# An attention stage whose tensor-engine order is written out by hand

## The chip, the cores and the metric

The kernel runs on one core of a Trainium2 chip. The metric is device microseconds of one launch. Engines are named as the profile names them: PE (matmul), DVE (vector), ACT (scalar), POOL (GpSimd) and SP, which issues the DMAs.

## What is computed

Two groups of tokens, a prompt of 1024 and a sample of 64 with a past of 512 keys, pass through two layers that share weights. The layer that matters here is the even one:

```python
q, k, v, ga, qi, ki, wi, gb, gc, xin, gz = split(h @ w_in)
score = sum_h wi[h] * relu(qi[h] @ ki.T)            # 8 index heads
keep  = the topk best keys of each query             # 256 for the prompt, 144 for the sample
p     = softmax(where(keep, q @ k.T / 8, -inf))      # 8 heads of 64, 2 key heads
a_out = (p @ v) * silu(ga)
b_out = gb * conv3(gc * xin) * silu(gz)
x    += gate * (concat(a_out, b_out) @ w_out)
```

A prompt query may see the keys of its own 64-chunk and of those before it. The odd layer (a gated projection, layer norm, a spatial product) follows and is not touched.

## The kernel before

Activations lie with features on the 128 partitions and all `TC` = 1088 tokens (1024 prompt, 64 sample) along the row. Every product is made of fp32r parts: a weight tile is split into `hi` and `lo` (ACT L238, POOL L239), the input into `ah` and `al`, and `project`/`steps` run three matmuls for each of 8 input tiles. With the three chunks of `CHUNKS` (364, 364 and 360 columns) one weight tile is 72 matmuls.

The work around the change, in order of the program:

- `topk` (DVE and ACT) finds each query's threshold for 7 score blocks `j`: six prompt blocks of 128 queries (b = 2 to 7, with 128(b+1) keys) and the sample's (576 keys). `mask` (L592 to L607, DVE but for one ACT step) then writes a block's additive bias into `self.bias`, through the scratch tile `self.cum`. Both live in the pool `search`.
- The pool `attn` opens when `search` closes, in the same memory. It holds the sample's keys `kc`, the query stacks `qst` (hi and lo parts of two heads, made by `pair_stack`: ACT L698, POOL L699), the parts `pth`/`ptl` of transposed probabilities (two buffers each) and the gate `ga`.
- Four head pairs `t` are attended, each in eight prompt blocks `b` (`ORDER[t]`) and the sample. `softmax` makes logits in chunks of at most 512 columns (PE L620), adds the bias and takes the maximum (DVE L622), exponentiates with a row sum (ACT L625), takes the reciprocal (DVE L626) and scales (POOL L627). `weighted` takes two key tiles at a time: four PE transposes into a PSUM bank (L650), the split into `pth` (ACT L276) and `ptl` (DVE L277), and the products with the values (PE L658). At the end of a block ACT copies the lower half out (L662) and DVE adds it (L722).
- Beside this run 11 projection tiles (`ATTN_TILES`: Q 1 to 3, GB 0 to 3, GA 0 to 3). They come from the generator `self.side`, one matmul at a time (PE L262): `BEFORE` = 435 of them ahead of the attention, then some at each `pace` call. A GA tile must wait until its head pair is done (`while kind == GA and self.done <= t: yield`): its evacuation copies the gate (ACT L909), applies Silu (L911) and multiplies into `self.q` (POOL L912), or for the last pair does it by chunks (L905, L906).
- Then `self.q` and `self.bo` are split into `ah`, `al` (L276, L277) and `out_projection` starts (PE L247, tile `op`).

PE, DVE, ACT and POOL each run their queue in order. A planner writes the order of all queues, by its own estimate of times and the order of the program; `pace` ties a few filler matmuls behind a given instruction (`issue_after`). PSUM has eight banks: `pj` 2, `lg` 3, `pt` 2, `av` 1.

Of the kernel before, what the change touches and what calls it, by code (L numbers as in the profile page):

```python
# [9 lines left out]
F32 = mybir.dt.float32  # L10
# [38 lines left out]
ATTN_TILES = [(Q_, 1), (Q_, 2), (Q_, 3), *((GB, t) for t in range(4)), *((GA, t) for t in range(4))]  # L49
# [38 lines left out]
BEFORE = 435  # L88
RATE = ((1, 1, 2),) * 4
# [8 lines left out]
class Trunk:  # L98
    def __init__(self, tc, ins, outs):
        self.tc, self.nc = tc, tc.nc  # L100
        self.i, self.o = ins, outs
        self.tags = ["pj"]

# [6 lines left out]
    def bank(self, tag, name):  # L110

        return self.ps.tile([P, 512], F32, tag=tag, name=name, bufs={"pj": 2, "lg": 3, "pt": 2, "av": 1}[tag])
# [137 lines left out]
    def steps(self, w, evac, chunks=range(NCH), n=2, tag="pj"):  # L250
# [3 lines left out]
        for c in chunks:  # L254
            a, b = CHUNKS[c]
            ps = self.bank(tag, "pj")[:, 0:b - a]
# [230 lines left out]
    def topk(self, pool):  # L487
# [11 lines left out]
        self.kneg = kneg = t("kneg")  # L499
# [11 lines left out]
        cv, m, sgn, limx, T, cand, flag = (t(n) for n in ("cv", "m", "sgn", "limx", "T", "cand", "flag"))  # L511
        self.T, self.cv, self.sgn = T, cv, sgn
        junks = [self.cum, pool.tile([P, SEQ], BF, name="junk")]
# [78 lines left out]
    def mask(self, pool, j):  # L592
# [14 lines left out]
        V.tensor_scalar(bi, bi, MASK, None, op0=OP.mult)  # L607


    def softmax(self, slot, lhs, keys, g, n, bias):  # L610

        nc = self.nc
        k, w = cut(n)
        p = self.S[:, slot:slot + n]
        st = self.small.tile([P, 4], F32, tag="sm", name="sm", bufs=8)
        for c in range(k):
            s = slice(c * w, (c + 1) * w)
            pt = self.bank("lg", "logit_ps")
            for i in range(2):
                mm = nc.tensor.matmul(pt[:, 0:w], lhs, keys[i][:, g, s], start=i == 0, stop=i == 1)  # L620
            self.pace(mm.ins, self.rate[0])
            nc.vector.tensor_tensor_reduce(out=p[:, s], in0=pt[:, 0:w], in1=bias[:, s], scale=-0.125,  # L622
                                           scalar=st[:, c - 1:c] if c else 3.0e38, op0=OP.add, op1=OP.min,
                                           accum_out=st[:, c:c + 1])
        nc.scalar.activation(p, p, AF.Exp, scale=-1.0, bias=st[:, k - 1:k], accum_out=st[:, 2:3])  # L625
        nc.vector.reciprocal(st[:, 3:4], st[:, 2:3])  # L626
        nc.gpsimd.tensor_scalar(p, p, st[:, 3:4], 0.0, op0=OP.mult, op1=OP.add)  # L627
        return p

    def weighted(self, pool, ps, g, n, vbase):  # L630

        nc = self.nc
        m = len(ps) * P
        av = self.bank("av", "av")
        nj = (n + P - 1) // P
        step = 512 // m
        for j0 in range(0, nj, step):
            js = range(j0, min(j0 + step, nj))
            full = [j for j in js if (j + 1) * P <= n]
            pt = self.bank("pt", "p_ps")  # L640
            hi = pool.tile([P, 512], F32R, tag="pth", name="pth", bufs=2)
            lo = pool.tile([P, 512], F32R, tag="ptl", name="ptl", bufs=2)
            for part in (full, [j for j in js if j not in full]):
                if not part:
                    continue
                r = min(P, n - part[0] * P)
                for j in part:
                    for i, p in enumerate(ps):
                        o = (j - j0) * m + i * P
                        mm = nc.tensor.transpose(pt[0:r, o:o + P], p[:, j * P:j * P + r], self.ident)  # L650
                if part is full:
                    self.pace(mm.ins, self.rate[2])
                x = slice((part[0] - j0) * m, (part[-1] + 1 - j0) * m)
                self.split(hi[0:r, x], lo[0:r, x], pt[0:r, x])
                for j in part:
                    o = (j - j0) * m
                    for i, t in enumerate((hi, lo)):
                        mm = nc.tensor.matmul(av[:, 0:m], self.vs[0:r, vbase + j, g, :], t[0:r, o:o + m],  # L658
                                              start=j == 0 and i == 0, stop=j == nj - 1 and i == 1)
            self.pace(mm.ins, self.rate[1])  # L660
        low = pool.tile([64, 256], F32, tag="avl", name="avl", bufs=2)
        nc.scalar.activation(low[:, 0:m], av[64:P, 0:m], AF.Copy)  # L662
        return av, low
# [38 lines left out]
    def sample_keys(self, pool):  # L702
        for g in range(2):
# [517 lines left out]
```

## Time and profile before

| | us |
|---|---|
| three runs | 1156.03, 1159.71, 1160.51 (median 1159.71) |
| profiled execution, its own time | 1157.27 |
| profiled execution, first to last instruction (span) | 1155.5 |
| mean granted TensorE clock | 0.983 |
| PE busy | 1100.1 |

Every sum below is made against the profiled execution: its own time is 1.77 us above its span, and the median of the runs is 2.44 us above its own time. A matmul's duration in the trace covers its way through the array; matmuls overlap, so what one costs in a row of them is the distance between starts. "Busy" is the union of such durations and hides part of the loss.

### The profile page before, as it was taken

The page shows a single profiled execution, that of the slowest core. Times are in us where ns is not written, and L with a number is a line of the kernel's source. Part 1 is how long each engine was busy: PE and PEld are TensorE (multiplying, and loading weights), DVE is VectorE, ACT ScalarE, POOL GpSimd, SP SyncE. Part 2 cuts the span into 40 slices and gives each one's busy share as a digit, 9 for nine tenths or more (in the row PEclk, how much of TensorE's full clock was granted, in tenths as well). Part 3 has the DMA queues.
Part 4 walks back from the last instruction along what each step waited for, and adds up shares of the span by engine and source line. Part 5 has one row for each costly group of instructions (what it writes and reads, how often), then busy time and mean ns, then how long its engine had stood idle before and what let it go on. Part 6 is the DMA issues. An engine that isn't in the chain of part 4 may idle for free.

```text
span 1155.5 us, 18886 instructions
## 1 busy us (share of the span) xinstructions
PE 1100.1 (95%) x7255; PEld 1051.7 (91%) x7255; DVE 670.9 (58%) x1657; ACT 516.8 (45%) x976; POOL 442.6 (38%) x454
## 2 busy tenths in 40 slices
PE   4899999999999979999898999999999999999997
PEld 4789689999999968888797999999999999999996
DVE  5712799998886998776666424411186064247134
ACT  5233686856777147777757313511221211135111
POOL 2633223466547165354523136521133211154222
PEclk9999999999999989998999999999999999999999
DMA  9746411211101110000000801011112111131012
GB/s 362 305 156 215 179 29 56 91 40 38 37 19 56 37 46 10 20 1 19 19 1 19 281 2 40 35 55 37 37 57 82 37 37 37 38 109 37 1 65 91
DMA packets 26074, 81.84 MB, mean 71 GB/s; under 512 B 3072, under 2 KB 9984, under 8 KB 23552
## 3 DMA queue, kind: packets, MB, share of 16 engines
q1 hardware_dynamic: 25984, 80.63, 19.8%
q8 instruction: 57, 0.93, 0.3%
q14 instruction: 33, 0.27, 0.1%
HBM read 74.50 MB, written 6.12 MB: 70 GB/s over the span
## 4 chain that ended last, share of the span: by engine, by line
PE 79%; DVE 8%; ACT 5%; issue 3%; POOL 2%; DMA 2%; SPq 0%; POOLq 0%; DVEq 0%; ACTq 0%
PE pj L247 40%; PE op L247 16%; PE pj L262 8%; PE av L658 3%; PE p_ps L650 2%; PE logit_ps L620 2%; PE ada_ps L153 2%; PE score_ps L427 1%; PE sgu_ps L1036 1%; PE first L318 1%; DVE cum L604 1%; PE score_ps L428 1%; POOL w_lo L239 1%; POOL hf L329 1%; ACT S L625 1%
## 5 line engine op out<-in xcount | busy, mean ns | idle before, releaser
L247 PE MATMUL pj<-ah,w_hi 128*128 128x364 f32 (+1 forms) x984 | 326.0, 331 | 1.0 <-ACT w_hi L238 1.0
L247 PE MATMUL pj<-al,w_hi 128*128 128x364 f32 (+1 forms) x984 | 323.8, 329 | 0.0
L247 PE MATMUL pj<-ah,w_lo 128*128 128x364 f32 (+1 forms) x984 | 323.1, 329 | 0.0
L239 POOL TENSOR_TENSOR w_lo<-w_raw,w_hi 128x1024 fp32r<-128x1024 f32 x63 | 159.1, 2527 | 351.2 <-ACT w_hi L238 350.8
L247 PEld LDWEIGHTS pj<-ah,w_hi 128*128 128x128 f32 x984 | 185.0, 188 | 2.0 <-ACT w_hi L238 1.3
L247 PEld LDWEIGHTS pj<-ah,w_lo 128*128 128x128 f32 x984 | 184.8, 188 | 0.3 <-issue 0.2
L247 PEld LDWEIGHTS pj<-al,w_hi 128*128 128x128 f32 x984 | 185.1, 188 | 0.0
L238 ACT ACTIVATE w_hi<-w_raw 128x1024 fp32r<-128x1024 f32 x69 | 72.9, 1058 | 135.7 <-PE pj L247 83.2
L247 PE MATMUL op<-ah,w_lo 128*128 128x448 f32 (+2 forms) x384 | 126.5, 330 | 3.0 <-POOL w_lo L239 3.0
L247 PE MATMUL op<-ah,w_hi 128*128 128x448 f32 (+2 forms) x384 | 127.1, 331 | 0.9 <-ACT ah L276 0.5
L247 PE MATMUL op<-al,w_hi 128*128 128x448 f32 (+2 forms) x384 | 126.4, 329 | 0.7 <-DVE al L277 0.7
L528 DVE TENSOR_SCALAR_CACHE_REDUCE cum<-S,cand 128x512 bf16<-128x512 f32 (+5 forms) x142 | 119.1, 838 | 2.0
L262 PE MATMUL pj<-ah,w_hi 128*128 128x364 f32 (+1 forms) x288 | 96.0, 333 | 6.6 <-DVE bo L894 5.6
L262 PE MATMUL pj<-al,w_hi 128*128 128x364 f32 (+1 forms) x288 | 96.4, 335 | 0.0
L262 PE MATMUL pj<-ah,w_lo 128*128 128x364 f32 (+1 forms) x288 | 95.7, 332 | 0.0
L976 DVE SCALAR_TENSOR_TENSOR x<-op,mod,x 128x192 f32<-128x192 f32 (+2 forms) x64 | 30.4, 497 | 104.9 <-PE op L247 102.5
L555 ACT ACTIVATE junk<-S,cand 128x896 bf16<-128x896 f32 (+2 forms) x78 | 77.7, 996 | 24.3 <-DVE m L558 20.5
L627 POOL TENSOR_SCALAR S<-S,sm 128x384 f32<-128x384 f32 (+8 forms) x68 | 50.4, 748 | 87.2 <-DVE sm L626 64.9
L247 PEld LDWEIGHTS op<-ah,w_lo 128*128 128x128 f32 x384 | 73.0, 190 | 5.5 <-POOL w_lo L239 3.3
L247 PEld LDWEIGHTS op<-ah,w_hi 128*128 128x128 f32 x384 | 73.0, 190 | 3.5 <-ACT ah L276 0.9
L247 PEld LDWEIGHTS op<-al,w_hi 128*128 128x128 f32 x384 | 73.0, 190 | 3.3 <-DVE al L277 1.1
L984 POOL TENSOR_TENSOR acc<-acc,sq 128x448 f32<-128x448 f32 (+2 forms) x40 | 39.2, 979 | 94.4 <-ACT sq L982 93.6
(242 smaller groups left out, 2001.3 us busy)
## 6 DMA issues: line engine op xcount, KB each, us to landing
w_raw<-in_w SPq DMA_DIRECT2D x53, 512.0 KB, 3.4
ada<-in_ada_w SPq DMA_DIRECT2D x19, 1024.0 KB, 9.1
w_raw<-in_wo SPq DMA_DIRECT2D x16, 512.0 KB, 3.5
x<-in_x SPq DMA_DIRECT2D x8, 544.0 KB, 6.6
bo<-in_ada_w SPq DMA_DIRECT2D x4, 1024.0 KB, 6.9
x<-in_x SPq DMA_DIRECT2D x1, 1792.0 KB, 9.5
out_y<-x SPq DMA_DIRECT2D x1, 1792.0 KB, 6.6
x<-in_x SPq DMA_DIRECT2D x1, 1536.0 KB, 9.4
```

Of the source, the lines that this page charges most:

```text
L153: nc.tensor.matmul(pt[32 * g:32 * g + 32, 0:P], self.cs[:, kt, :], raw(kt)[:, g * P:(g + 1) * P], start=kt == 0, stop=kt == KT - 1, tile_p ...
L238: nc.scalar.activation(hi, raw, AF.Copy)
L239: (nc.gpsimd if lo_eng == "pool" else nc.vector).tensor_sub(lo, raw, hi)
L247: last = self.nc.tensor.matmul(ps, wt[:, kt, :], at[:, kt, c0:c1], start=n == 0, stop=n == len(mms) - 1)
L262: self.nc.tensor.matmul(ps, wt[:, kt, :], at[:, kt, a:b], start=kt == 0 and i == 0, stop=kt == KT - 1 and i == 2)
L528: V.tensor_scalar(junks[0][:, 0:SW[j]], self.S[:, span(j)], thr, 0.0, op0=OP.is_lt, op1=OP.add, accum_out=col(cv, j))
L555: nc.scalar.activation(junks[1][:, 0:SW[j]], self.S[:, span(j)], AF.Sign, scale=-1.0, bias=col(cand, j), accum_out=col(cv, j))
L620: mm = nc.tensor.matmul(pt[:, 0:w], lhs, keys[i][:, g, s], start=i == 0, stop=i == 1)
L627: nc.gpsimd.tensor_scalar(p, p, st[:, 3:4], 0.0, op0=OP.mult, op1=OP.add)
L658: mm = nc.tensor.matmul(av[:, 0:m], self.vs[0:r, vbase + j, g, :], t[0:r, o:o + m], start=j == 0 and i == 0, stop=j == nj - 1 and i == 1)
L976: nc.vector.scalar_tensor_tensor(x[:, t, a:b], ps[:, a:b], self.mod[l][:, 16 + t, j:j + 1], x[:, t, a:b], op0=OP.mult, op1=OP.add)
L984: nc.gpsimd.tensor_add(acc, acc, sq)
```

## The change

Only the stage between `topk` and the output projection of the even layer changes, and on PE alone the order is now that of the program (`manual_schedule`); the other queues are still written by the planner.

- Attention is a loop over slots. A slot is a group of two key tiles of one block: 20 slots for a head pair, 80 in all. Iteration g issues on PE: the transposes of slot g, logits of blocks whose first slot comes about `LEAD` = 3 later, `FILL` filler matmuls (2.6, 5.5, 5.5 and 3.5 a slot in the four head pairs), and the value products of slot g - `LAG` (2).
- The sample of all four head pairs is attended first, with 45 filler matmuls a pair, and the masks of the prompt blocks are issued behind the sample's mask on DVE. `cum` moves from `search` into the buffer of `ga`; `kc` no longer lies over it. `BEFORE` is 255.
- Gates: `0.5 * p` in the scaling, and `(1 + tanh(ga / 2)) * ga` from PSUM by ACT and DVE. A GA tile may run during its own head pair, the multiplication into `q` follows in `through`.
- Query stacks exist twice; the second one takes the sample's key buffer once the sample is done. The stack of the next head pair is made at the third block of the present one.
- One of `lg`'s banks is shared (`x`), so that in the attention `av` has two banks and `lg` two.
- The split and the output projection of the even layer start with the `bo` half (`OUT_KTS`).

The diff, cut to its core (the functions it replaces are printed above):

```diff
-ATTN_TILES = [(Q_, 1), (Q_, 2), (Q_, 3), *((GB, t) for t in range(4)), *((GA, t) for t in range(4))]
+ATTN_TILES = [(Q_, 1), (Q_, 2), (Q_, 3), (GB, 0), (GB, 1), (GB, 2), (GA, 0), (GA, 1), (GB, 3), (GA, 2), (GA, 3)]
-BEFORE = 435
-RATE = ((1, 1, 2),) * 4
+BEFORE = 255
+FILL_S = (22, 12, 11)
+FILL = (2.6, 5.5, 5.5, 3.5)
+LEAD, LAG = 3, 2
+OUT_KTS = (4, 5, 6, 7, 0, 1, 2, 3)
     def bank(self, tag, name):
+        if tag == ("av" if self.attending else "lg"):
+            self.turn += 1
+            if self.turn % (2 if self.attending else 3) == 0:
+                tag = "x"
+        return self.ps.tile([P, 512], F32, tag=tag, name=name, bufs={"pj": 2, "lg": 2, "pt": 2, "av": 1, "x": 1}[tag])
+    def logits(self, it, e, c):
...
+        for i in range(2):
+            nc.tensor.matmul(pt[:, 0:w], lhs, keys[i][:, t // 2, s], start=i == 0, stop=i == 1)
+        nc.vector.tensor_tensor_reduce(out=p[:, s], in0=pt[:, 0:w], in1=bias[:, s], scale=-0.125,
...
+        if c == k - 1:
+            nc.scalar.activation(p, p, AF.Exp, scale=-1.0, bias=st[:, c:c + 1], accum_out=st[:, 2:3])
+            nc.vector.reciprocal(st[:, 3:4], st[:, 2:3])
+            nc.gpsimd.tensor_scalar(p, p, st[:, 3:4], 0.5, op0=OP.mult, op1=OP.mult)
+    def transposes(self, pool, it, js):
...
+        pt = self.bank("pt", "p_ps")
+        hi = pool.tile([P, 512], F32R, tag="pth", name="pth", bufs=2)
+        lo = pool.tile([P, 512], F32R, tag="ptl", name="ptl", bufs=2)
...
+                    nc.tensor.transpose(pt[0:r, o:o + P], p[:, j * P:j * P + r], self.ident)
...
+            self.split(hi[0:r, x], lo[0:r, x], pt[0:r, x])
+    def weighted(self, pool, it, js, parts):
...
+        if (js[-1] + 1) * P >= n:
+            low = pool.tile([64, 256], F32, tag="avl", name="avl", bufs=2)
+            nc.scalar.activation(low[:, 0:m], av[64:P, 0:m], AF.Copy)
+            for e in range(2):
+                s = slice(e * w, (e + 1) * w)
+                nc.vector.tensor_add(self.q[64 * e:64 * e + 64, t, o:o + w], av[0:64, s], low[:, s])
+    def exact_queries(self, dst, t, a, b, step):
...
+                nc.scalar.activation(d[h, s] if step > DEC else d[h], x, AF.Copy)
+                nc.gpsimd.tensor_sub(d[l, s] if step > DEC else d[l], x, d[h, s] if step > DEC else d[h])
+    def queries(self, pool, t):
+        if t == 1:
+            self.st.append([pool.tile([P, 2 * NS], F32R, tag=f"kc{e}", name=f"st{e}")[:, 0:SEQ] for e in range(2)])
+        self.exact_queries(lambda e: self.st[t % 2][e], t, 0, SEQ, 512)
+    def attend_sample(self, pool):
...
+        for t in range(4):
+            it = (t, "s")
+            for e, c in self.chunks(it):
+                self.logits(it, e, c)
+            fill(FILL_S[0])
+            js = self.groups(it)
+            parts = [self.transposes(pool, it, j) for j in js]
+            fill(FILL_S[1])
+            for j, p in zip(js, parts):
+                self.weighted(pool, it, j, p)
+            fill(FILL_S[2])
+    def attend(self, pool, through):
+        items = [(t, b) for t in range(4) for b in ORDER[t]]
...
+        for g in range(int(ahead[0][0]), len(slots) + LAG):
+            if 0 <= g < len(slots):
+                it, js = slots[g]
+                waiting.append((it, js, self.transposes(pool, it, js)))
+                if it[0] < 3 and js[0] == 0 and it[1] == ORDER[it[0]][2]:
+                    self.queries(pool, it[0] + 1)
+            while ahead and ahead[0][0] <= g:
+                self.logits(*ahead.pop(0)[1:])
+            credit += FILL[min(max(g, 0), len(slots) - 1) // (len(slots) // 4)]
+            while credit >= 1:
+                credit -= 1
+                next(self.side, None)
+            if waiting and (len(waiting) > LAG or g >= len(slots)):
+                it, js, parts = waiting.pop(0)
+                self.weighted(pool, it, js, parts)
+                if it[1] == ORDER[it[0]][-1] and (js[-1] + 1) * P >= self.keys_of(it):
+                    through(it[0])
...
-                for j in range(NSB):
-                    self.mask(se, j)
...
+                self.cum = ap.tile([P, 2 * TC], BF, tag="ga", name="cum")
...
-                        nc.scalar.activation(g[:, cols(c)], ps, AF.Copy)
-                        if c == NCH - 1:
-                            nc.scalar.activation(g, g, AF.Silu)
-                            nc.gpsimd.tensor_mul(q, q, g)
+                        g = ga[0][:, cols(c)]
+                        nc.scalar.activation(g, ps, AF.Tanh, scale=0.5)
+                        nc.vector.scalar_tensor_tensor(g, g, 1.0, ps, op0=OP.add, op1=OP.mult)
...
-                        while kind == GA and self.done <= t:
+                        while kind == GA and self.done < t:
...
+                def through(t):
+                    while (GA, t) in left:
                         next(self.side)
+                    if t < 3:
+                        nc.gpsimd.tensor_mul(q, q, ga[0])
+                    else:
+                        for c in range(NCH):
+                            s = slice(*OUT_CHUNKS[c])
+                            nc.vector.tensor_mul(q[:, s], q[:, s], ga[0][:, s])
                     self.done = t + 1
+                self.sample_keys(ap)
+                self.tags = ["pj", "pj", "lg", "lg", "lg"]
+                with self.tc.manual_schedule(engines={mybir.EngineType.PE}):
+                    for _ in range(BEFORE):
+                        next(self.side)
+                    self.attending, self.tags = True, ["pj"]
+                    self.mask(NSB - 1)
+                    self.attend_sample(ap)
+                    for j in range(NSB - 1):
+                        with self.tc.issue_after(self.masked):
+                            self.mask(j)
+                    self.queries(ap, 0)
+                    self.attend(ap, through)
...
-                self.product(ps[:, 0:w], ws[t], a0, b0)
+                self.product(ps[:, 0:w], ws[t], a0, b0, range(KT) if l else OUT_KTS)
```

## Rows read from the trace of the kernel before

**Rows 1.** Windows: stretch, length, busy us (instructions) by engine, granted clock, DMA.
```profile
344.93:379.35 34.42, 34.42 (x208) 34.42 (x208) 25.14 (x100) 27.22 (x52) 23.50 (x29) 1.00 0.15 47
379.35:425.00 45.65, 40.08 (x232) 39.43 (x230) 45.54 (x57) 6.21 (x9) 17.38 (x7) 0.96 0.11 38
455.00:475.00 20.00, 19.61 (x136) 18.02 (x134) 16.00 (x51) 12.93 (x26) 7.49 (x8) 1.00 0.08 27
515.00:535.00 20.00, 17.76 (x90) 15.15 (x89) 11.27 (x37) 14.15 (x28) 9.63 (x9) 0.74 0.09 27
535.00:565.00 30.00, 29.41 (x197) 27.05 (x196) 22.25 (x74) 22.07 (x51) 13.10 (x14) 1.00 0.00 1
```

**Rows 2.** Windows of L262 alone (filler): length, PE busy (matmuls), weight loads, clock.
```profile
455.00:475.00 20.00, 6.98 (x31) 4.72 (x29) 1.00 0.08 27
515.00:535.00 20.00, 2.67 (x9) 1.94 (x10) 0.74 0.09 27
535.00:565.00 30.00, 13.44 (x63) 10.00 (x63) 1.00 0.00 1
```

**Rows 3.** Waits, 379 to 635 us: who waited for whom: us, times, longest.
```profile
ACT kc L709 <- DVE bias L606: 16.4, 1, 16.4
```

**Rows 4.** The chain that ended last, 600 to 640 us: start, us, what.
```profile
622.51 1.28 PE pj L262 x6
...
629.83 4.95 POOL w_lo L239
...
634.82 5.31 PE op L247 x18
```

**Rows 5.** Timeline of PE, 461.9 to 463.1 us: start us, us, engine line operation.
```profile
461.94 1.03 PE L650 MATMUL p_ps<-ident,S 128*128 128x128 f32 x8
462.73 0.36 PE L658 MATMUL av<-pth,vs 128*128 128x256 f32 x1
462.94 0.28 PE L658 MATMUL av<-ptl,vs 128*128 128x256 f32 x1
463.06 0.28 PE L658 MATMUL av<-pth,vs 128*128 128x256 f32 x1
```

**Rows 6.** Lines of 379 to 635 us: group xcount | busy us, mean ns | idle before.
```profile
L277 DVE TENSOR_TENSOR ptl<-p_ps,pth 128x512 fp32r<-128x512 f32 (+1 forms) x88 | 53.8, 620 | 20.6 <-ACT pth L276 19.7
L722 DVE TENSOR_TENSOR q<-av,avl 64x128 f32<-64x128 f32 x64 | 17.9, 280 | 7.9 <-ACT avl L662 7.3
L626 DVE RECIPROCAL sm<-sm 128x1 f32<-128x1 f32 x68 | 10.6, 160 | 15.8 <-ACT S L625 15.1
L625 ACT ACTIVATE S<-S,sm 128x384 f32<-128x384 f32 (+8 forms) x68 | 52.3, 769 | 7.7 <-DVE sm L622 6.5 <-POOL S L627 0.9
L276 ACT ACTIVATE pth<-p_ps 128x512 fp32r<-128x512 f32 (+1 forms) x88 | 46.8, 539 | 33.9 <-PE p_ps L650 18.5 <-PE av L658 14.8
L911 ACT ACT_TABLE_LOAD x3 | 3.8, 1283 | 0.1
L627 POOL TENSOR_SCALAR S<-S,sm 128x384 f32<-128x384 f32 (+8 forms) x68 | 50.4, 748 | 87.2 <-DVE sm L626 64.9 <-PE p_ps L650 16.9 <-PE av L658 4.6
L699 POOL TENSOR_TENSOR qst<-q,qst 64x512 fp32r<-64x512 f32 (+1 forms) x16 | 24.8, 1558 | 4.1 <-DVE sm L626 2.2 <-ACT qst L698 1.1
```

**Rows 7.** Windows of L622 alone: length, DVE busy us (instructions), clock.
```profile
425.00:635.00 210.00, 57.12 (x208) 0.94 0.05 15
```

**Rows 8.** Windows of L650 alone (transposes): length, PE busy (matmuls), weight loads, clock.
```profile
455.00:475.00 20.00, 6.07 (x42) 4.86 (x42) 1.00 0.08 27
535.00:565.00 30.00, 7.14 (x48) 5.76 (x48) 1.00 0.00 1
```

**Rows 9.** Tile ckr: the four loads of the sample's keys, issue to landing.
```profile
DMA to landing us min/median/max: 2.0/2.2/3.5
```

**Rows 10.** Lines of DVE by form, 379 to 440 us: one mask step at two widths.
```profile
L606 DVE SCALAR_TENSOR_TENSOR bias<-S,T,bias 128x512 bf16<-128x512 f32 x1 | 2.8, 2770 | 0.0
L606 DVE SCALAR_TENSOR_TENSOR bias<-S,T,bias 128x576 bf16<-128x576 f32 x1 | 0.8, 806 | 0.0
```

More of the change, by code (lines that the diff above doesn't have):

```diff
@@ L248, in product, with steps @@
         return last.ins
-    def steps(self, w, evac, chunks=range(NCH), n=2, tag="pj"):
+    def steps(self, w, evac, chunks=range(NCH), n=2, tag=None):
         hi, lo = w
@@ L498, in topk @@
         steps, upper = 23, 7
-        self.kneg = kneg = t("kneg")
+        cv, sgn, T, kneg = (self.keep.tile([P, NSB], F32, name=n) for n in ("cv", "sgn", "T", "kneg"))
+        self.T, self.cv, self.sgn, self.kneg = T, cv, sgn, kneg
         lims, lad = t("lims", 4 * NSB).rearrange("p (i j) -> p i j", i=4), t("lad", steps)
@@ L606, in mask, with chunks, groups @@
         V.scalar_tensor_tensor(bi, sl, thr, bi, op0=OP.is_lt, op1=OP.add)
-        V.tensor_scalar(bi, bi, MASK, None, op0=OP.mult)
-    def softmax(self, slot, lhs, keys, g, n, bias):
+        self.masked = V.tensor_scalar(bi, bi, MASK, None, op0=OP.mult).ins
+    def chunks(self, it):
+        return [(e, c) for e in range(1 if it[1] == "s" else 2) for c in range(cut(self.keys_of(it))[0])]
+    def groups(self, it):
+        step = 4 if it[1] == "s" else 2
+        n = (self.keys_of(it) + P - 1) // P
+        return [range(j, min(j + step, n)) for j in range(0, n, step)]
@@ L612, in softmax, with keys_of @@
+    def keys_of(self, it):
+        return NS if it[1] == "s" else P * (it[1] + 1)
+    def logits(self, it, e, c):
         nc = self.nc
+        t, b = it
+        n = self.keys_of(it)
         k, w = cut(n)
[L614 to L630, printed above, removed]
+        if b == "s":
+            lhs, keys, bias = self.both[t], self.kc, self.bias[:, SOFF[-1]:SOFF[-1] + n]
+        else:
+            lhs, keys = self.st[t % 2][e][:, b * P:(b + 1) * P], self.kp
+            bias = self.corner[:, 256 - n:256] if b < 2 else self.bias[:, SOFF[b - 2]:SOFF[b - 2] + n]
@@ L632, in weighted @@
+        if c == k - 1:
[3 more added lines that the diff above has]
+    def transposes(self, pool, it, js):
         nc = self.nc
+        n = self.keys_of(it)
+        ps = [self.p[it, e][0] for e in range(1 if it[1] == "s" else 2)]
         m = len(ps) * P
[L634 to L635 removed]
@@ L636, in weighted @@
[L636 to L660, printed above, removed]
@@ new lines, in attend @@
+    def attend(self, pool, through):
+        items = [(t, b) for t in range(4) for b in ORDER[t]]
+        slots, first = [], {}
+        for it in items:
+            first[it] = len(slots)
+            slots += [(it, js) for js in self.groups(it)]
+        ahead, due = [], float(len(slots))
+        for it in reversed(items):
+            due = min(due, first[it] - LEAD + 0.75)
+            for x in reversed(self.chunks(it)):
+                due -= 0.75
+                ahead.insert(0, (due, it, *x))
+        waiting = []
+        credit = 0.0
+        for g in range(int(ahead[0][0]), len(slots) + LAG):
[15 more added lines that the diff above has]
+                    through(it[0])
```

123 lines of the change are left out of this document (61 added, 62 removed).

## The prediction

> **What bounds the kernel now.** PE is busy 1100.1 of 1155.5 us, so the first question is what that busy time is worth. I first read the windows of the stage [rows 1]. From 344.93 us 208 filler matmuls take 34.42 us: 0.1655 us each, or 0.455 ns a column, at full clock. This is PE at its pace. From 379.35 to 425 PE is still 88% busy while DVE works 45.54 of 45.65 us: that is the masks and eight evacuations. From 515 to 535 PE is 89% busy, but at a mean clock of 0.74; from 565 to 585 it is the same again. The filler view shows what the engine did there: 9 filler matmuls in 20 us, against 31 in 455 to 475 and 63 in the 30 us from 535, both at full clock [rows 2]. A GA tile must wait for its head pair, so filler runs dry near the end of pairs 1 and 2, PE waits for softmax steps, and the clock falls to its 1.2 GHz level for about half of such a stretch.
>
> The waits name the loss ahead of the attention: ACT stood 16.4 us at `kc`, whose memory is the masks' scratch, until a mask step of DVE [rows 3]. All ACT work of the attention was queued behind. The chain of waits names the loss at the end: after the last GA tile's matmuls (622.51 us) come splits and a 4.95 us `w_lo`, and the output projection starts at 634.82 [rows 4].
>
> **The floor.** Call T the start of the output projection; before, T is 634.8. What follows T is 1155.5 - 634.8 = 520.7 us and stays. From 344.93 PE needs:
> - 11 tiles x 72 = 792 filler matmuls x 0.1655 = 131.1;
> - logits: each pair has 4 x 4608 prompt and 2 x 576 sample columns, in all 78336 x 0.455 ns = 35.6;
> - 308 transposes: eight of them take 462.73 - 461.94 = 0.79 us [rows 5], so 0.099 each, 30.5;
> - value products: 288 x 0.12 us (462.94 to 463.06 [rows 5]) and 40 of half the width at 0.06: 37.0.
>
> The sum is 234.2 us, and the stage takes 289.9: 55.7 us are lost. The change alters no count, so PE's floor for T is 579.1.
>
> **PE in the new order.** `BEFORE`: 255 x 0.1655 = 42.2, to 387.1 us. Sample: per pair 0.5 logits, 0.5 transposes, 0.6 products and 45 filler, 9.1 us, four times 36.3. A head pair's own work is 8.4 + 7.1 + 8.6 = 24.2 us, 1.21 a slot. With filler (52 matmuls by credit and 17 when `through` finishes GA 0; 110; 106; 72) the four pairs are 35.6, 42.4, 41.7 and 36.1.
>
> **DVE in the new order.** Per head pair: splits 80/88 of 53.8 / 4 = 12.2, adds 17.9 / 4 = 4.5, reciprocals 16 x 0.16 = 2.6 [rows 6], bias and maximum 96/104 of 57.12 / 4 = 13.2 [rows 7]: 32.5. Sample: 3.0 a pair (two L622 of 0.55, two splits, two adds, a reciprocal), 12.0. Gate steps on PSUM, which no row shows: at the split's 0.62, 1.9 a GA tile; its ends are 0.28 (the narrow add) and 0.77 (the exponential), so 0.8 to 2.3, and all of it lies in DVE's queue.
> The sample's mask now goes first, and the rest of the masks share DVE with the sample and pair 0. Up to the end of pair 0 DVE has 45.5 + 12.0 + 1.9 + 32.5 = 91.9 us from 379.35, PE 71.9 from 387.1. DVE ends later: 471.3 without a gap. In a chained stretch DVE was busy 80% at most (16.00 of 20 [rows 1]), beside the masks 100%; I take 0.85 for the chained part, 34.4 / 0.85 = 40.5, so pair 0 ends at 379.35 + 57.5 + 40.5 = 477.4.
>
> **Pairs 1 to 3.** Pairs 1 and 2 are PE's: 84.1 us of work. How well PE runs with softmax beside it: 42 transposes are 11.7 slots at 3.6 a slot, 14.1 us, with 31 filler 19.2 of 20 us, or 0.96; from 535 the same sum is 26.5 of 30, 0.88 [rows 2, 8]. At 0.92 these pairs take 91.4. In pair 3 DVE (34.4 / 0.85 = 40.5) is a little later than PE (36.1 / 0.92 = 39.2). T = 477.4 + 91.4 + 40.5 = 609.3.
>
> **The rest of the edits.**
> - Sample keys: four loads through one buffer, each 2.2 us to landing [rows 9] and then at most 0.54 on ACT and 1.56 on POOL (nearest rows, L276 and L699 [rows 6]). They move ahead of weight loads on SP, whose tile is 72 matmuls, 11.9 us, ahead. Pairs 0 and 1 need two of the four: 8.6 us from the end of the search at 379, against 387.1 for PE's first logits. Between nothing and 5 us; I take nothing, since the first load can land before 379.
> - Query stacks: per pair four ACT copies and four POOL steps of 1.56, 6.2 us on POOL, queued among the scalings (0.75 [rows 6]). A block's chain is 0.55 + 0.77 + 0.16 + 0.75 = 2.2 us, and logits are issued 3 slots (5 to 6 us) ahead: a 1.56 us step fits in between. Without that lead it costs its 1.56, up to 16 times.
> - Gates: three Silu of a whole tile with three loads of a table each way (3.8 us a group [rows 6]) leave ACT. Both pairs of loads lay in the stretches without filler, whose loss the floor already counts.
> - PE's fixed order adds waits: a transpose that waits for POOL's scaling or for a free `pt` bank holds logits, filler and products behind it, and DVE, ACT and POOL wait for those. That is the 0.92, and a rival below.
> - Second `av` bank, `bo` first in the projection: after the last product the chain to `ah` and `al` (copy, adds, gate, two splits, some 2.7 us at 0.28 to 0.77 each) is covered by the first 12 matmuls of 448 columns, 2.4 us. The 4.95 us `w_lo` goes behind the attention's end, beside the 4.9 us of the first output tile. If that cover is gone, 3 to 5 us.
>
> The span becomes 609.3 + 520.7 = 1130.0, its own time 1131.8, and with the 2.4 us by which the median stands above, 1134.
>
> **A rule that speaks against it.** One mask step took 2770 ns at 512 columns and 806 at 576 [rows 10], while POOL was busy 17.38 us of that window [rows 1]: DVE lost time beside POOL, and the 45.5 us hold that loss. The Trainium skill (SBUF — State Buffer, "SBUF: two separate sides") says that DVE and GpSimd lock a shared port pair for a whole instruction and the loser waits. By it alone, a DVE step on SBUF would lose up to all of POOL's time. As a mechanism of this kernel it is a rival below.
>
> **The rivals.**
> - PE near its floor: DVE keeps up everywhere. 387.1 + 192.1 / 0.96 = 587.2, so 1112. For it: DVE's 45.5 hold that POOL loss. Against it: DVE's 91.9 us. Chance 0.12.
> - It doesn't do what it says: only PE's order is by hand, and the planner puts the masks ahead of the sample's steps. The sample's maxima then start at 424.9, PE stands from 387.6, and 424.9 + 36.3 + (35.6 + 120.2) / 0.92 = 630.6: 1155. Against it: the sample comes earlier in the program. 0.11.
> - Tanh needs another table than the exponential: 12 chunks x 2 x 1.283 us = 31 us on ACT [rows 6], of which some 20 would hold exponentials up past the lead: 1154. No Tanh stands in this trace. 0.05. The Trainium skill (ScalarE: Activation LUTs, "Table sets: the hidden batching unit") lists tanh in the set of exp; by that, none of it.
> - Slower, by the two `pth`/`ptl` buffers: the split of slot g waits for the products of g - 2, at the end of iteration g; transposes g + 2 wait for that split. Two slots then last 0.54 + 0.62, what is queued ahead of these on ACT and DVE, and PE's own 2.1: a slot is 1.63 + q / 2. T stays at 634.8 if a slot takes (634.8 - 387.1 - 36.3) / 80 = 2.64, from q = 2.0 on. With two exponentials and two maxima ahead (q = 2 x 0.77 + 2 x 0.55 = 2.64) a slot is 2.95, T 659: 1184. For it: queues in order, and PE can no longer pull other work forward. Against it: 1.71 us a slot in 455 to 475, with the same number of buffers. 0.11.
> - Slower, by POOL's port: DVE loses all of POOL's time up to the end of pair 0, 17.4 + 50 x 7.49 / 20 = 36 us [rows 1]: 1170. 0.04.
>
> **How the numbers follow.** The forecast, 1134, has 0.57. Its own range: DVE without a gap to the end of pair 0 and PE at 0.96 gives T = 471.3 + 125.2 = 596.5, 1121; DVE at 0.74 (22.25 of 30 [rows 1]), PE at 0.88 and 5 us for the keys gives 379.35 + 57.5 + 46.5 + 95.6 + 46.5 + 5 = 630.5, 1155. I take 1118 to 1157: part of the first rival lies below, most of the two slower ones above. About 0.5% is what a measurement can tell from no change, 1154 to 1165 here: faster 0.78 (the forecast, PE at its floor, the table, and 0.04 of the planner's case), same 0.09 (its other 0.07 and 0.02 of the two slower rivals), slower 0.13 (what is left of these).
>
> **What would show it.** Right: no ACT wait of 16 us at `kc`; DVE full from 379 until pair 0; no stretch of several us at the lower clock between 500 and 600; one table load for the whole stage; projection at about 609. Wrong: PE waiting for `ptl` in most slots, masks ahead of the sample's L622, table loads around each Tanh, or a late `w_lo` after T.

## The result, and the profile after

The changed kernel takes 1169.72 us (median; 1167.88 to 1173.34) against 1157.91 us for the kernel before on the same chip (four runs, the three named above and 1156.12): a ratio of 1.0104, 95% interval 1.0069 to 1.0139. It is 1% slower, more than the interval leaves to chance, where 1134 and "faster" were forecast. The profiled execution took 1167.88 us, its span is 1166.1.

The first view is the windows by stage: the wait ahead of the sample, the sample, pair 0, pairs 1 and 2, pair 3 with the tail. They answer [rows 1].

```profile
core 0: us, PE busy (x) PEld busy (x) DVE busy (x) ACT busy (x) POOL busy (x), PEclk, DMA share, GB/s
387.15:396.50 9.35, 0.16 (x1) 0.03 (x1) 9.14 (x9) 0.42 (x1) 6.44 (x6) 0.62 0.04 15
396.50:458.50 62.00, 48.35 (x257) 45.93 (x257) 41.28 (x76) 15.41 (x34) 18.55 (x17) 0.87 0.07 22
458.50:504.00 45.50, 42.62 (x286) 39.37 (x285) 36.07 (x120) 35.40 (x77) 23.05 (x26) 1.00 0.04 13
504.00:604.00 100.00, 93.93 (x641) 90.25 (x640) 72.66 (x229) 66.25 (x144) 46.05 (x44) 1.00 0.07 22
604.00:646.70 42.70, 33.60 (x222) 31.38 (x222) 34.82 (x90) 29.10 (x69) 10.85 (x13) 0.98 0.00 1
```

The output projection goes on at 646.7 us, not at 609.3, and what follows takes 519.4 us, as before (520.7). So the whole miss lies ahead of it, and the stages name it: the forecast had PE end the sample at 423.4 (it ends at 458.5: +35.1), which leaves 54.0 for pair 0 up to its 477.4 (45.5: -8.5), pairs 1 and 2 91.4 (100.0: +8.6), and the rest 40.5 (42.7: +2.2). The sum is +37.4.

The waits of PE from 379 to 460 us (engine and line, who was waited for, total us, times, longest):

```profile
PE logit_ps L656 <- ACT kc L290: 9.2, 1, 9.2
PE p_ps L682 <- POOL S L663: 8.9, 4, 3.0
PE av L700 <- DVE ptl L291: 4.6, 1, 4.6
```

The wait for `kc` is not that of [rows 3]: there ACT waited for a mask step; here the timeline of ACT and POOL shows a queue.

```profile
382.90 0.82 ACT L743 ACTIVATE qs<-q 64x64 fp32r<-64x64 f32 x3
383.75 2.60 ACT L743 ACTIVATE st<-q 64x512 fp32r<-64x512 f32 x4
386.37 0.42 ACT L290 ACTIVATE kc<-ckr 128x256 fp32r<-128x256 f32 x1
...
386.81 6.02 POOL L744 TENSOR_TENSOR st<-q,st 64x512 fp32r<-64x512 f32 x4
392.91 0.92 POOL L291 TENSOR_TENSOR kc<-ckr,kc 128x256 fp32r<-128x256 f32 x1
...
395.94 0.42 ACT L290 ACTIVATE kc<-ckr 128x256 fp32r<-128x256 f32 x1 [9.15 <-DMA ckr<-in_ck]
```

Pair 0's query stack (`st`), which the program issues after the sample and which is first needed at 458 us, was put ahead of the sample's keys: 2.60 us on ACT and 6.02 on POOL. Only when POOL's step at 392.91 had read `ckr` could the next piece be loaded into that one buffer, and ACT's second `kc` came at 395.94.

The wait for `ptl`, one of the four for `S`, and the tail's are in the timeline around 408, 451 and 643 us:

```profile
402.55 0.81 DVE L620 SCALAR_TENSOR_TENSOR bias<-cum,bias 128x640 bf16<-128x640 bf16 x1
...
404.46 0.75 POOL L663 TENSOR_SCALAR S<-S,sm 128x576 f32<-128x576 f32 x1 [3.60 <-DVE sm L662]
...
408.84 2.34 POOL L251 TENSOR_TENSOR w_lo<-w_raw,w_hi 128x1024 fp32r<-128x1024 f32 x1 [2.87 <-ACT w_hi L250]
408.92 3.08 DVE L620 SCALAR_TENSOR_TENSOR bias<-cum,bias 128x768 bf16<-128x768 bf16 x1
411.92 0.87 DVE L291 TENSOR_TENSOR ptl<-p_ps,pth 128x512 fp32r<-128x512 f32 x2
412.65 0.33 PE L700 MATMUL av<-ptl,vs 128*128 128x128 f32 x1 [4.59 <-DVE ptl L291]
...
434.31 0.42 DVE L622 TENSOR_SCALAR bias<-bias 128x1024 bf16<-128x1024 bf16 x1
...
445.42 5.10 POOL L744 TENSOR_TENSOR st<-q,st 64x512 fp32r<-64x512 f32 x4 [7.29 <-ACT st L743]
450.61 0.75 POOL L663 TENSOR_SCALAR S<-S,sm 128x576 f32<-128x576 f32 x1
451.42 1.33 PE L682 MATMUL p_ps<-ident,S 128*128 128x128 f32 x5 [3.04 <-POOL S L663]
...
643.35 2.34 POOL L251 TENSOR_TENSOR w_lo<-w_raw,w_hi 128x1024 fp32r<-128x1024 f32 x1 [10.88 <-ACT w_hi L250]
643.66 2.52 DVE L1017 TENSOR_TENSOR q<-q,ga 128x448 f32<-128x448 f32 x1
646.10 0.52 DVE L987 SCALAR_TENSOR_TENSOR ga<-ga,pj 128x360 f32<-128x360 f32 x1
646.67 0.74 PE L259 MATMUL op<-ah,w_hi 128*128 128x448 f32 x1 [4.73 <-DVE ga L987]
```

The sample's split (`ptl`, L291) stands on DVE behind mask steps, and PE, whose order is fixed, stands with it. The scaling of `S` waits for DVE's reciprocal in the same way at 404. The last mask step is the one at 434.31, so the last wait for `S`, 3.0 us at 451, is not the masks': pair 1's query stack, first needed in pair 1, stands ahead of the scaling on POOL. The tail answers [rows 4]: the projection waits for a gate step that stands behind a long product on DVE.

### The profile page after: what moved, and what is told of

Its sections match the earlier page's. It is cut to its first block, busy times and chain, and to the rows that moved or that the text cites. A ratio compares the mean times of both kernels' runs of the same rounds, so it can differ in the third digit from the quotient of the medians.

```text
span 1166.1 us, 18874 instructions
## 1 busy us (share of the span) xinstructions
PE 1093.5 (94%) x7255; PEld 1051.1 (90%) x7255; DVE 678.7 (58%) x1661; ACT 512.2 (44%) x976; POOL 443.8 (38%) x462
## 4 chain that ended last, share of the span: by engine, by line
PE 52%; DVE 4%; issue 2%; POOL 1%; ACT 1%; DMA 1%; POOLq 0%; DVEq 0%; ACTq 0%
PE pj L259 23%; PE op L259 16%; PE pj L276 4%; PE p_ps L682 3%; PE logit_ps L656 2%; PE av L700 2%; PE sgu_ps L1127 1%; DVE al L291 1%; DVE ptl L291 1%; DVE S L657 1%; PE v_ps L1173 1%; DMA w_raw<-in_wo 1%; POOL w_lo L251 1%; POOL S L663 0%; ACT pth L290 0%
## 5 line engine op out<-in xcount | busy, mean ns | idle before, releaser
L251 POOL TENSOR_TENSOR w_lo<-w_raw,w_hi 128x1024 fp32r<-128x1024 f32 x63 | 155.7, 2473 | 348.0 <-ACT w_hi L250 347.7
L543 DVE TENSOR_SCALAR_CACHE_REDUCE junk<-S,cand 128x512 bf16<-128x512 f32 (+5 forms) x142 | 119.0, 838 | 2.0
L663 POOL TENSOR_SCALAR S<-S,sm 128x128 f32<-128x128 f32 (+8 forms) x68 | 51.7, 767 | 85.5 <-DVE sm L662 75.1
```

Of the source, the lines that this page charges most:

```text
L251: (nc.gpsimd if lo_eng == "pool" else nc.vector).tensor_sub(lo, raw, hi)
L543: V.tensor_scalar(junks[0][:, 0:SW[j]], self.S[:, span(j)], thr, 0.0, op0=OP.is_lt, op1=OP.add, accum_out=col(cv, j))
L663: nc.gpsimd.tensor_scalar(p, p, st[:, 3:4], 0.5, op0=OP.mult, op1=OP.mult)
```

## The experiments

Each kernel ran against the kernel before on the same chip. Ratios are to that kernel; the changed kernel's is 1.0104, so 0.01 below it is some 11.6 us. The chips differ (the kernel before has medians of 1157.9 to 1160.3 us on them), so compare kernels by ratio. "Logits" are the first of the sample and of pair 0, "projection" is where it goes on after the last value product (us). By then 42 of its matmuls have run in e6 to e10 and e12, and 21 in the others; the 21 between are some 4.3 us of work at 0.455 ns a column.

| kernel | median us | ratio, 95% interval | logits sample, pair 0 | projection |
|---|---|---|---|---|
| changed | 1169.7 | 1.0104 (1.0069 to 1.0139) | 396.5, 458.5 | 646.7 |
| e1 keys first | 1163.9 | 1.0034 (1.0019 to 1.0050) | 387.1, 454.5 | 642.6 |
| e2 fill moved | 1165.6 | 1.0051 (1.0033 to 1.0068) | 397.1, 454.1 | 645.1 |
| e3 lag one | 1158.3 | 0.9990 (0.9976 to 1.0003) | 398.7, 462.7 | 640.0 |
| e4 no masks | 1152.4 | 0.9939 (0.9917 to 0.9962) | 396.3, 441.7 | 629.8 |
| e5 Silu | 1188.2 | 1.0259 (1.0232 to 1.0287) | 396.8, 460.4 | 666.1 |
| e6 planner | 1141.1 | 0.9844 (0.9819 to 0.9869) | 399.5, 439.3 | 622.0 |
| e7 mixed, lag one | 1141.5 | 0.9845 (0.9823 to 0.9868) | 431.3, 416.9 | 625.6 |
| e8 mixed, lag two | 1156.7 | 0.9978 (0.9965 to 0.9992) | 430.9, 416.1 | 639.0 |
| e9 planner, lag one | 1143.3 | 0.9874 (0.9847 to 0.9901) | 402.1, 441.8 | 627.2 |
| e10 mixed, planner | 1146.8 | 0.9903 (0.9877 to 0.9929) | 434.3, 417.1 | 629.9 |
| e11 one stack | 1164.0 | 1.0048 (1.0031 to 1.0065) | 396.2, 457.1 | 645.3 |
| e12 early gate | 1171.1 | 1.0118 (1.0085 to 1.0150) | 396.4, 461.0 | 655.8 |
| e13 three together | 1147.0 | 0.9897 (0.9868 to 0.9925) | 386.7, 448.3 | 627.1 |
| e14 mixed, late gate | 1143.8 | 0.9864 (0.9836 to 0.9891) | 431.2, 416.4 | 624.1 |

**e1, the keys first.**

```diff
-            for o in range(0, PAST, 256):
-                raw = pool.tile([P, 256], F32, tag="ckr", name="ckr", bufs=1)
-                self.load(raw, self.i["ck"][g, :, o:o + 256])
+            raw = pool.tile([P, 512], F32, tag="pth", name="ckr", bufs=2)
+            self.load(raw, self.i["ck"][g])
...
-                    self.queries(ap, 0)
+                    with self.tc.issue_after(self.keys[0]), self.tc.issue_after(self.keys[1]): self.queries(ap, 0)
```

> The changed kernel, with the sample's keys ahead of pair 0's query stack on ACT and POOL, and loaded as two pieces of 512 columns into the two pth buffers, not as four through one. In the changed kernel PE waits 9.20 us for kc (387.0 to 396.5), and then runs filler at half clock until 403. Theory A (the late keys are a loss of their own): the wait falls to at most 1 us, the output projection starts 9 to 12 us earlier, 1158 to 1161. Rival (the sample is held by its softmax chains and by the mask steps on DVE, and PE only meets them sooner): the time moves into waits for S and ptl in the same stage, 1166 to 1170.

The wait for `kc` is gone (0.7 us), and the sample starts 9.4 us earlier; pair 0 starts only 4.0 earlier. PE's waits from 379 to 460 us in this kernel:

```profile
PE p_ps L682 <- POOL S L663: 18.3, 4, 6.4
PE logit_ps L656 <- POOL kc L291: 0.7, 1, 0.7
```

The waits for `S` grew by 9.4 us, to 18.3, while the 4.6 us for `ptl` went: PE waits 19.0 us in all, 22.7 before. The softmax chain has DVE steps, and PE now meets the masks sooner. By the ratios it is 0.7% faster, some 8 us; the two profiled executions differ by 4.4. The time lies between the two expectations, the trace is nearer to the rival's.

**e2, the filler dealt otherwise:** `BEFORE = 311`, `FILL_S = (31, 0, 0)`.

> The changed kernel with the same 435 filler matmuls, dealt otherwise: 311 ahead of the sample (255 before), and in each sample pair 31 between logits and transposes (22), none after the transposes (12) and none after the products (11). Theory A (PE's written order leaves too little work where the waits are): the 9.2 us wait for kc is covered by 56 filler (9.3 us), the 8.9 us of waits for S shrink by 9 x 0.166 x 4 = 6 us, and the products wait at most 4 x 1.2 us for their splits: 8 to 14 us faster than the changed kernel, 1155 to 1161. Rival (the masks on DVE set the pace): what is gained before the first logits comes back as waits for ptl, within 4 us of the changed kernel.

The filler covers the wait for `kc`, but then the second logits wait 7.1 us for the first one's maximum, which stands behind masks on DVE; the waits for `S` fall to 1.9 us (8.9), those for the split's two halves grow to 7.4 (4.6). The rival describes it, though the maximum and not `ptl` is what PE waits for. Pair 0 starts 4.4 us earlier, and 2.8 of this are lost again before the projection. By the ratio it is some 6 us faster than the changed kernel, by the spans 2.2: between the two expectations.

**e3, the lag:** `LEAD, LAG = 3, 1`.

> The changed kernel with the value products one slot behind the transposes (two). With two, the split of a slot needs buffers that the products of two slots earlier still read, and these stand at the end of the same iteration. Theory B (the two buffers of pth and ptl hold the pairs up): the transposes' waits for ptl (0.8, 3.6, 1.5 and 2.2 us in the four pairs) go, and the pairs get 6 to 10 us shorter, 1159 to 1163. Rival (the wait is the latency of copy and split itself): the wait moves from the transposes to the products of the slot, within 3 us of the changed kernel, or up to 5 us slower.

From pair 0's first logits to the projection it takes 177.3 us against 188.2: 10.9 us less, although PE's waits for the split only fall from 8.3 to 2.8 us there. The direct evidence stands on ACT. First the costliest line of the copies in the changed kernel from 387 to 647 us, then the same line in this one (busy, mean ns, idle ahead of it by releaser):

```profile
L290 ACT ACTIVATE pth<-p_ps 128x512 fp32r<-128x512 f32 (+1 forms) x88 | 47.1, 540 | 38.9 <-PE av L700 22.1 <-PE p_ps L682 13.2 <-DVE sm L657 2.5
```

```profile
L290 ACT ACTIVATE pth<-p_ps 128x512 fp32r<-128x512 f32 (+1 forms) x88 | 46.7, 539 | 26.4 <-PE p_ps L682 25.3
```

ACT's copy stood 22.1 us until value products of two slots earlier had freed a buffer; with a lag of one it only waits for its own transposes. The sample takes 2.0 us longer here, so the projection comes 6.7 us earlier; the time, 1158.3 us, is just below theory B's range.

**e4, without the prompt's masks:** `for j in range(0):` around the six masks, and the bias set to zero.

> The changed kernel without the six masks of the prompt's blocks (their bias is set to zero early by one POOL step); the sample's mask is still computed. This takes some 40 us of steps from DVE between 385 and 435. Theory A (late keys, queues of ACT and POOL): the wait of 9.2 us for kc stays, only the 4.6 us for ptl and some of the 8.9 us for S go, 1160 to 1166. Rival (DVE's masks hold the sample): sample stage near 45 us against 72, 1145 or less.

```profile
386.90:396.30 9.40, 0.74 (x6) 0.47 (x4) 0.00 (x0) 0.42 (x1) 5.46 (x5) 0.65 0.21 70
396.30:441.70 45.40, 42.12 (x257) 40.59 (x258) 13.68 (x44) 15.63 (x34) 16.16 (x17) 0.96 0.09 30
441.70:629.80 188.10, 170.16 (x1147) 160.98 (x1145) 143.61 (x437) 130.30 (x288) 79.65 (x81) 1.00 0.05 15
```

The windows (columns as above) settle two things. The sample stage falls from 62.0 to 45.4 us, so 16.6 us of it are the masks beside it, and the clock is back at 0.96. And what follows takes 188.1 us, as with masks (188.2): the masks, which end before pair 0 begins, do not touch the pairs. The time is below theory A's range and above its rival's; both causes are there. Of the 16.6, 10.5 are waits that go (13.5 for `S` and `ptl` fall to 3.0), and some 6 are the clock's, an estimate from 0.13 of 62.0 and 0.04 of 45.4. The wait for `kc` has nothing to do with the masks: it stays (8.7 us). The 3.0 that are left for `S` are the wait behind pair 1's query stack.

**e5, Silu in place of tanh.**

```diff
-                        nc.scalar.activation(g, ps, AF.Tanh, scale=0.5)
-                        nc.vector.scalar_tensor_tensor(g, g, 1.0, ps, op0=OP.add, op1=OP.mult)
+                        nc.scalar.activation(g, ps, AF.Silu)
```

> The changed kernel with its gates as one Silu on ACT each (12 chunks), the scaling by 1 and no gate step on DVE: tanh undone. If Silu needs another table than the exponential, ACT gets up to 24 table loads of 1.28 us, 31 us in all, in a stage where it is busy about 70%: each holds exponentials up by 2.6 us, as long as the lead of three slots hides that, nothing, otherwise 5 to 20 us; I expect some of it, 1175 to 1185. Rival (ACT has slack and the DVE gate steps cost as much as they save): within 4 us of the changed kernel.

The groups of ACT from 387 to 667 us show the price:

```profile
L661 ACT ACT_TABLE_LOAD x12 | 15.4, 1283 | 1.1 <-DVE sm L657 1.0
L986 ACT ACT_TABLE_LOAD x12 | 15.4, 1283 | 0.6 <-PE pj L276 0.5
```

With tanh there is one load in the whole stage. PE's waits for `ptl` after 460 us are 23.2 us (8.1). So the change of the gates is worth some 18 us in this order by the ratios (19.9 by the spans), a little more than I expected.

**e6, the planner's order:** the statement that fixes PE's order (`manual_schedule`) left out, nothing else.

> The changed kernel with PE's order left to the planner, as the other engines' is; the program's order is the same. Theory (PE's fixed order costs, since one late S or kc holds everything behind it): the planner pulls filler and logits of pair 0 into the sample's waits, sample and pair 0 get 10 to 20 us shorter, 1150 to 1160. Rival (the order by hand is worth what it costs: the planner runs filler out early, as in the kernel before, and ends with stretches at the lower clock): 1170 or slower.

```profile
379.35:399.50 20.15, 18.05 (x107) 17.48 (x106) 19.76 (x23) 7.33 (x17) 14.46 (x12) 1.00 0.18 59
399.50:439.30 39.80, 37.15 (x227) 34.88 (x226) 38.54 (x68) 14.48 (x31) 20.31 (x15) 1.00 0.10 34
439.30:622.00 182.70, 174.38 (x1140) 156.80 (x1138) 141.28 (x445) 129.98 (x291) 79.29 (x82) 1.00 0.05 16
```

This is the strongest single result: the same work on the same engines, 2.6% faster than the changed kernel and 1.6% faster than the kernel before. From the sample's first logits to pair 0's it takes 39.8 us (62.0) at a clock of 1.00 (0.87); the pairs take 182.7 (188.2), although 21 more matmuls of the projection run among them. It is also faster than the 1150 to 1160 that I expected. DVE still works 38.54 of those 39.8 us: the masks are as much in the way, but PE does other work meanwhile. The helpers are as late as before: the masks end at 435.1 us (434.7), and ACT makes the second piece of `kc` at 397.7 (395.9); so it is PE's order that gains, not theirs. The rival's filler did run out early, at 593 us, but the clock was 1.00 in each 20 us window from 380 to 620.

**e7 and e8, the sample among pair 0's blocks,** with a lag of one and of two.

```diff
-BEFORE = 255
+BEFORE = 430
-FILL = (2.6, 5.5, 5.5, 3.5)
+FILL = (2.6, 5.5, 5.5, 4.5)
...
-        items = [(t, b) for t in range(4) for b in ORDER[t]]
+        items = [*FIRST, *((t, b) for t in range(1, 4) for b in ORDER[t])]
```

> The sample's four items among the blocks of pair 0 (after blocks 1, 2, 3 and 4) in place of a stage of their own, 430 filler matmuls ahead (255) so that the masks run beside them, value products one slot behind, and 4.5 filler a slot in pair 3 (3.5). If the separate sample stage is the loss: PE starts pair 0 at 344.9 + 430 x 0.1655 = 416, and pairs with the sample's own 6.5 us take the 177 us of the run with lag one and 7 more, so the output projection starts at about 600, and the time is 1122 to 1130. Rival (masks and sample share DVE wherever the sample stands, so pair 0 only starts after the masks' end near 425, and the waits for S come back in it): 1140 to 1155.

> The same as the run with the mixed sample, with products two slots behind as in the changed kernel. If the two buffers of pth and ptl cost what the lag run showed (10.9 us over the four pairs), it is 9 to 13 us slower than the mixed run with lag one. Rival (the lag only mattered behind the late sample): within 3 us of it.

The windows of e7, and below its longest wait between 416 and 440 us:

```profile
380.00:416.80 36.80, 36.80 (x223) 36.80 (x222) 36.10 (x44) 10.52 (x21) 18.84 (x15) 1.00 0.17 55
416.80:431.30 14.50, 4.10 (x18) 3.54 (x17) 14.29 (x23) 2.12 (x6) 1.77 (x2) 0.65 0.00 0
431.30:625.60 194.30, 184.82 (x1234) 174.84 (x1233) 151.83 (x470) 139.84 (x313) 89.88 (x92) 0.98 0.05 17
```

```profile
PE logit_ps L657 <- DVE sm L658: 10.4, 1, 10.4
```

PE is ready at 416.8 and finds DVE busy 14.29 of 14.5 us, mostly with masks, which end at 433.3: my 1122 to 1130 left that out, and the rival's mechanism holds at its lower end. Still it is 2.6% faster than the changed kernel, though not by one edit: lag, filler and the place of the sample differ. With lag two the projection comes 13.4 us later and the median is 15.2 us higher, so the buffers' cost shows here too, above the 9 to 13 expected.

**e9 and e10, the planner with the lag, and with the mixed sample.**

> PE's order left to the planner, and value products one slot behind. If the two buffers of pth and ptl cost their 11 us under any order: 1130 to 1136. Rival (the planner already pulls other work into the wait for them; 2.5 us of waits for ptl are left with it against 8.4): within 4 us of the planner's 1141.

> The mixed sample with lag one, PE's order left to the planner. By hand it waited 10.4 us for the maxima behind the masks, near 420 to 430, with the clock at 0.74 there. If that is the fixed order's, the planner keeps filler for it: 1122 to 1132. Rival (430 filler ahead leave too little for the rest, under any order): 1138 to 1146.

Neither gains. e9 fits its rival: where the planner can fill the waits for the split, the shorter lag brings nothing. e10 is slower than e7, 1146.8 us, just past its rival's range. PE's longest wait for a maximum behind the masks falls to 3.4 us there (10.4 by hand), so the theory had the wait right, and yet nothing comes of it. The last filler runs at 598.5 us (610.6 in e7), as the rival has it; but in e6 it runs at 593.2, so this alone does not explain the loss, and the cause stays open.

**e11, one query stack.**

```diff
-            lhs, keys = self.st[t % 2][e][:, b * P:(b + 1) * P], self.kp
+            lhs, keys = self.st[0][e][:, b * P:(b + 1) * P], self.kp
```

with the stack written ahead of the next pair's first logits.

> The changed kernel with one query stack for all pairs, written again after the last logits of the pair before and ahead of the first logits of the next. Prediction's step: the two stacks cover four ACT copies and four POOL steps a pair; without them the first logits of a pair wait for at least one copy, one POOL step and their queues, 4 to 6 us three times, less what the lead of three slots hides: 5 to 15 us slower than the changed kernel, 1175 to 1185. Rival (the lead hides all of it): within 4 us.

The second stack gains nothing here: the kernel without it is some 6 us faster by the ratio and 1.0 by the spans, and the lead hides what it should have cost. The wait of 3.0 us for `S` at 451 is gone, as no second stack is made ahead of the sample's last scaling, and pair 0 starts 1.4 us earlier.

**e12, the last gate earlier:** `FILL = (2.6, 5.5, 5.5, 4.5)`.

> The changed kernel with 4.5 filler a slot in the last pair (3.5), so that the last gate tile ends four slots earlier. The output projection waits 4.7 us for the gate step of its last chunk, which stands on DVE behind a 2.52 us product. If the tail's cover was lost to that order, the wait falls to about 1 us: 3 to 5 us faster than the changed kernel, 1164 to 1167. Rival (w_lo on POOL or the last softmax chains hold the tail as long): within 2 us of it.

No gain, as the rival has it. The waits from 600 to 657 us:

```profile
PE op L259 <- DVE ga L987: 2.8, 1, 2.8
PE op L259 <- ACT ah L290: 2.4, 1, 2.4
```

The 4.7 us became 2.8 and 2.4, the last slots had no filler, and the last value product came 11.8 us later; some 4.3 us of this are the 21 matmuls of the projection that moved ahead of it.

**e13, three changes together, in the written order:** keys first, lag one, `FILL_S = (31, 7, 7)`.

> The changed kernel, still in its written order, with three of its waits removed together: the sample's keys first (as in the run with keys first), products one slot behind, and of the 180 filler of the sample stage 31 a pair ahead of the transposes, 7 and 7 behind (22, 12, 11). Theory (the written order loses by separate waits, each of which can be taken away): the gains add, 4 to 8 by the keys, 11 by the lag, 4 to 6 by the filler: 1145 to 1153. Rival (one resource, DVE with the masks, sets the sample stage, and a wait removed there comes back as another; only the lag, in the pairs, is separate): 1155 to 1160.

```profile
386.70:448.30 61.60, 47.24 (x258) 44.39 (x257) 50.25 (x84) 14.81 (x33) 24.73 (x20) 0.89 0.06 18
448.30:627.10 178.80, 169.59 (x1147) 162.17 (x1145) 141.75 (x437) 130.38 (x288) 79.62 (x81) 0.98 0.05 16
```

The time is in the theory's range, and the gains add up: pair 0 starts 10.2 us earlier and the rest is 9.4 us shorter. But the sample itself still takes 61.6 us; only its start moved. Of the stage itself the rival is right.

**e14, mixed with the changed kernel's filler rate.**

> The mixed sample with lag one, and 3.5 filler a slot in the last pair, as in the changed kernel (4.5). With 4.5 the last filler ended 12 us ahead of the last value product, and the clock was 0.83 in 610 to 630. If the end of pair 3 needs filler more than the projection needs an early gate: 3 to 6 us faster than the mixed run, 1135 to 1139. Rival (the gate step on DVE is late again, as in the changed kernel, and costs its 4 to 5 us): 1140 to 1145.

The rival holds: the last value product ends 3.9 us earlier (619.4 against 623.3), but that is no more than the 4.3 us of the projection's matmuls that no longer run ahead of it; the wait for the gate step is 5.7 us again (0.2), and the time is the same within the intervals.

## Why the prediction was wrong

**The step that failed is the sample at PE's pace, 36.3 us, "four times 9.1".** It costed PE's instructions and no wait, as if PE could do something else while a chain was late, and the change had taken just that away. The 36.3 is no addend of the 609.3. It made PE's path to the end of pair 0, 71.9 us from 387.1 and so to 459.0, look shorter than DVE's to 477.4, and the sum went by DVE's. The run went by PE's: 9.35 us for `kc`, 62.0 for the sample and 45.5 for pair 0 are 116.9 from 387.15, to 504.0. The 62.0 are 36.3 of work, 13.5 of waits for `S` and `ptl`, some 8.1 by the clock (an estimate, 62.0 x 0.13), and 4.1 that I can't assign. e4 shows that 16.6 us hang on the masks, e6 that 17 to 22 hang on PE's fixed order (22.2 less the 5 us of 30 matmuls that lie outside the stage there). The two overlap: with the masks and PE free the stage takes 39.8 us, with PE fixed and no masks 45.4.

**The sample's keys, "between nothing and 5 us; I take nothing".** I asked when the loads land. The first was early; the second waited for the one buffer, and so for ACT's and POOL's queues, where pair 0's query stack stood ahead. PE stood 9.2 us. The step counted one step on ACT and one on POOL for each load, and nothing that could stand ahead of them. With e1 the projection came 4.1 us earlier; the longer waits for `S` took the rest back.

**DVE up to the end of pair 0: 91.9 us, ending at 477.4.** This is the path that the sum took, and the list of signs had DVE full until pair 0. DVE was busy 7.8 to 9.9 us of each 10 until 430, the masks ended at 434.7, and then it worked 3.0 and 2.6 us of the two 10 us windows from 440, since PE's order had filler and the sample's last chains in front of pair 0's logits. In pair 0 DVE was busy 36.07 of 45.5 us, and e4 shows that the masks no longer matter there. First the masks held DVE, and then PE's order held the stage; I had let DVE hold it to the end.

**Pairs 1 and 2 at 0.92** took 100.0 us for 84.1 of work, 0.84. The rival of the two `pth`/`ptl` buffers was the right mechanism with too high a deciding point: a slot was 188.2 / 80 = 2.35 us, below 2.64, and it cost 10.9 us over the four pairs all the same (e3), 13.4 beside a mixed sample (e8). It had 0.11 as a case of its own; as a term it belonged into the sum.

**The tail, "3 to 5 us" without its cover,** was 4.7 us, near the upper bound. The cover of 12 matmuls did not help, as the gate step and not the chain after the last product came late.

**What was right.** No wait of 16 us for the masks' memory stands at `kc`; the clock is 1.00 from 460 to 604; there is one table load in the stage. The Trainium skill (ScalarE: Activation LUTs, "Table sets: the hidden batching unit") lists tanh in the set of exp, and this load agrees. e5 puts the worth of tanh in this order, with a gate for each chunk, at 18 us; I had set nothing for it, since the few loads of the kernel before lay in stretches that were lost anyway. The lead covers the making of a query stack, as the prediction says; but the second stack gained nothing and, made during the sample, brought the wait of 3.0 us at 451, which e11 does not have. The planner did not put the masks ahead of the sample, it interleaved them, which was bad enough. The port did not cost the 36 us of its rival: all masks together, with what the port adds to them, cost 16.6.

**What stays open.** Inside the sample stage the masks' 16.6 us were not divided between DVE's queue and the slower steps beside POOL; e13 leaves 61.6 us there, and no run tried the masks after the sample.

## What to carry to other kernels

Where an engine's order is written out, cost each chain that it waits for, not only its own instructions: the same program with that one order left to the planner was 2.6% faster. Where a buffer is freed by a step that the same order puts later, the number of buffers and the lag are one choice: one slot less of lag gave 10.9 us without any memory in the written order, and nothing under the planner (e9). And when a step is moved forward, read the queues of the helpers for steps that nobody needs yet: two query stacks, each made too early, stood ahead of the sample's keys and of its last scaling.

## What the runs showed of the hardware

The clock can fall after a short idle time of PE, and the filler behind it takes longer. Windows of 4 us in the changed kernel around the waits at 408, 435 and 448 us:

```profile
408.00:412.00 4.00, 0.06 (x1) 0.00 (x0) 3.97 (x3) 0.76 (x1) 2.34 (x1) 1.00 0.00 0
412.00:416.00 4.00, 3.35 (x14) 3.12 (x15) 3.94 (x10) 0.28 (x1) 0.00 (x0) 0.65 0.42 135
416.00:420.00 4.00, 4.00 (x16) 4.00 (x15) 1.85 (x4) 0.51 (x2) 0.36 (x1) 0.50 0.01 2
...
436.00:440.00 4.00, 1.81 (x13) 1.81 (x14) 0.43 (x1) 0.75 (x2) 2.13 (x2) 1.00 0.37 124
440.00:444.00 4.00, 4.00 (x27) 3.85 (x27) 1.42 (x5) 0.28 (x1) 0.00 (x0) 1.00 0.04 11
...
448.00:452.00 4.00, 0.96 (x6) 0.66 (x5) 0.36 (x2) 0.00 (x0) 3.23 (x3) 0.84 0.00 0
452.00:456.00 4.00, 4.00 (x24) 3.96 (x22) 0.88 (x2) 0.75 (x2) 0.00 (x0) 0.73 0.00 0
```

After 4.6 us of idle PE, to 412.65, the granted clock was 0.65 and 0.50 in the next two windows, so at its 1.2 GHz level for most of them; filler matmuls start 0.30 us apart there, and 0.17 at full clock. The length of the idle time does not settle it in this trace: after 3.0 us, to 438.2, the clock stayed at 1.00, and after another 3.0, to 451.4, it was at the lower level for part of the two windows (0.84 and 0.73).

A DVE step with two operands in SBUF that overlapped POOL's `w_lo` ended late: the mask step L620 took 3.08 us beside a `w_lo` of 2.34, and 0.81 without it at 640 columns; the gate product L1017 took 2.52 beside 2.34, and 0.55 without it at 384. They ended 0.81 and 0.48 us after `w_lo`, near the time that such a step takes alone, as if they had begun when it was nearly done. The Trainium skill (SBUF — State Buffer, "SBUF: two separate sides") says that such a step and a POOL step lock a shared port pair for a whole instruction; these rows agree. The prediction's "a DVE step on SBUF" was wider than that. In the tail this is some 2 of the 4.7 us, an estimate from 2.52 and 0.55.
